# Fewer idle products in the last expert group, an earlier first sum over tokens, and a split first weight half

## The chip, the cores and the metric

One core of a Trainium2 chip runs the whole program. The metric is the device time of one execution in microseconds (us); less is better.

## What is computed

Two transformer blocks on one sequence of 256 tokens with 1024 features, all in float32. The first block mixes tokens (attention and a short convolution) and then runs a mixture of 32 SwiGLU experts: each token picks one of four router groups and two of the eight experts in it. The second block starts with a projection of the first block's result `x` onto five parts (q, k, v, u, z) of 512 columns each, and ends with a dense SwiGLU layer. Cut to the part that matters here:

```python
for g in range(N_GROUPS):
    act = silu(einsum('nd,edf->nef', h, w_gate[sl])) * einsum('nd,edf->nef', h, w_up[sl])
    act = act * combine[:, g, :, None]
    y = y + einsum('nef,efd->nd', act, w_down[sl])
x = x + y                                   # end of the first block
h = x @ w_in_2                              # start of the second: (256, 1024) @ (1024, 2560)
q, k, v, u, z = split(h, ...)
```

## The kernel before

**Experts.** The kernel takes the 32 experts four at a time: `group(g, ...)` runs eight times (g = 0 to 7; 7 is the last group, called `end` in the code). Each expert has room for 32 tokens, so that a group is one 128-wide gathered tile `xg`. A group's weights come as twelve tiles of 1 MB: eight "gu" tiles (gate and up columns, one for each 128 rows of the 1024 features, the loop over `kc`), and four "dn" tiles (the down projection: two column halves `c`, two row halves `f`). `by_expert` (L815) multiplies one weight tile by the four experts' tokens on TensorE (PE): L819. I call the tiles of the last group gu0 to gu7 and dn0 to dn3 (dn0 and dn1 make column half 0, dn2 and dn3 half 1).

After the eight gu tiles, ScalarE (ACT) and VectorE (DVE) make `h` (L848, L849), PE transposes it (L853), ACT copies it to `hT` (L854), and the dn tiles follow. The result of a column half is copied to `y` (half 0: ACT, L877; half 1 in the last group: ACT and DVE, a half each, L872 and L873). `to_tokens(c)` (L859, eight passes on PE) multiplies `y` by the group's scatter matrix and adds it onto four accumulators `acc` in PSUM, two feature chunks of 128 each: `acc[0]` and `acc[1]` get column half 0, `acc[2]` and `acc[3]` half 1. After the last group `acc` holds `x`, transposed.

**Idle products.** In the last group PE also runs products of the identity with itself into a bank that nobody reads (`warm`, L239): six (`WARM2`) after each of the eight gu tiles and six after dn0 and dn1. A float32 product of this kind shows as two passes in the trace.

**Start of the second block.** Its weights and `x` are used as sums of two float32r parts. `hi_lo` makes them: ACT copies the high part (L266), DVE subtracts for the low part (L267). `hi_lo_here` is the same at a fixed place in the order (L271, L272). `W.ahead(n)` splits weight units (half a tile, 128x1024) up to the n-th. PE's products of the projections are all on L284; the first one, z ("z2"), takes four units of 12 products each.

**Order and data.** PE, ACT and DVE run here in the order in which the code is written. All weight tiles come through one list on the SP queue (L79): a tile is issued as soon as a buffer is free and the transfer eight places before it has landed. Of the second block's tiles, z's first one is loaded in two halves of 512 KB.

Of the kernel before, what the change touches and what calls it, by code (L numbers as in the profile page):

```python
# [19 lines left out]
KD = D // P  # L20
# [14 lines left out]
WBUF = 3  # L35
WBUF2 = 9
WARM0 = 14
WARM1 = (18, 6)
WARM2 = 6

VEC = {}
_at = 0
# [84 lines left out]
def fused_blocks(ctx: ExitStack, tc: tile.TileContext, a, out):  # L127
# [10 lines left out]
    def pool(name, bufs=1, side=None, **kw):  # L138
        es = ExitStack()
        p = es.enter_context(tc.tile_pool(name=name, bufs=bufs, side=side, reuse_waits="tile", **kw))  # L140
        return es, p


    units_a, units_b, order = [], [], []
# [59 lines left out]
    def bank():  # L204
        return pa.tile([P, 512], F32, tag="a", name="pa_t")
# [7 lines left out]
    def bank_c():  # L213
        return pc.tile([P, 512], F32, tag="c", name="pc_t")
# [6 lines left out]
    feed = Feed(nc, order)  # L221
# [10 lines left out]
    ident = cp.tile([P, P], F32, name="ident")  # L232
    make_identity(nc, ident)

    def warm(new, n, x):

        z = new()[:, 0:P]
        for _ in range(n):
            tc.keep_in_program_order(mm(z, ident, x, start=True, stop=True))  # L239
# [25 lines left out]
    def hi_lo(hi, lo, src):  # L265
        act(hi, src, AF.Copy)  # L266
        tt(out=lo, in0=src, in1=hi.bitcast(F32), op=ALU.subtract)  # L267

    def hi_lo_here(hi, lo, src):

        tc.keep_in_program_order(act(hi, src, AF.Copy))  # L271
        tc.keep_in_program_order(tt(out=lo, in0=src, in1=hi.bitcast(F32), op=ALU.subtract))  # L272
# [31 lines left out]

    def proj_tok(W, name, xh, xl, then={}, new=bank):
        accs = [[new()] for _ in range(NT)]
        for u in range(4):
            hi, lo = W.get(name)
            for t in range(NT):
                dense_tok(accs[t], [(2 * u, hi, lo, 0), (2 * u + 1, hi, lo, 512)], (0,), xh, xl, t, u == 0, u == 3)  # L310
            if u in then:
                W.ahead(W.n_got + W.lead)
                then[u]()
        return [c[0] for c in accs]

    def rows_proj(W, name, acc, xh, xl, k0, first, last, then={}):

        if not last:
            for u in range(2):
                hi, lo = W.get(name)  # L320
                for t in range(NT):
                    dense_tok(acc[t], [(k0 + u, hi, lo, 0)], (0, 1), xh, xl, t, first and u == 0, False)
                if u in then:
                    W.ahead(W.n_got + W.lead)
                    then[u]()
            return
        ks = [(k0 + u,) + W.get(name, 2 * u) + (0,) for u in range(2)]
        for t in range(NT):
            for c in range(2):
                dense_tok(acc[t], ks, (c,), xh, xl, t, first, True)  # L330
                if 2 * t + c in then:
                    then[2 * t + c]()

    def four_banks():
        return [[bank(), bank()] for _ in range(NT)]
# [22 lines left out]
    def hb(x):  # L358
# [4 lines left out]
    xh, xl, at_hl, y_hl = [ringx.tile([P, 2048], F32, tag="w", name=n).bitcast(F32R).rearrange("p (k s) -> p k s", k=KD)  # L363
                           for n in ("xh", "xl", "at_hl", "y_hl")]
    ath, atl = at_hl[:, 0:4, :], at_hl[:, 4:8, :]
    yh, yl = y_hl[:, 0:4, :], y_hl[:, 4:8, :]
    wes, wp = pool("w_a", bufs=WBUF, side="left")
# [5 lines left out]
    c0, c1 = slice(0, 512), slice(512, D)  # L373
# [14 lines left out]
    W = Split(feed, wp, units_a, two_halves, WBUF)  # L388
# [190 lines left out]
    acc = None  # L579
    merged = {}  # L580
    with tc.manual_schedule(engines={mybir.EngineType.PE}):
        for i in range(4):
# [7 lines left out]
            for b, n, h_, l_ in ((1, "cv", yh, yl), (0, "sb", ath, atl)):  # L590
                z = bank_c()
                hi, lo = W.get(n)
# [10 lines left out]
            if i:  # L603
                acc = acc or four_banks()
# [168 lines left out]
    def scatter(g, pg):  # L773

        pc = pg.rearrange("p t (e s) -> p t e s", e=GE)
        tt(out=pc, in0=pc,
           in1=comb[:, :, GE * g:GE * g + GE].unsqueeze(3).to_broadcast([P, NT, GE, SLOT]), op=ALU.mult)
        st = dp.tile([P, S], F32, tag="st", name="st", bufs=2)
        zs = bank_c()[:, 0:S]
        for t in range(NT):  # L780
            tr(zs[:, t * P:(t + 1) * P], pc[:, t].rearrange("p e s -> p (e s)"), ident)
        act(st, zs, AF.Copy)
        return st
# [28 lines left out]
    acc = [bank().rearrange("p (k s) -> p k s", k=2) for _ in range(4)]  # L812
    slots = [slice(e * SLOT, (e + 1) * SLOT) for e in range(GE)]

    def by_expert(outs, x, w, start, stop):  # L815
        n = 512 // len(outs)
        for i, out in enumerate(outs):
            for e, sl in enumerate(slots):
                mm(out[sl, 0:n], x[:, sl], w[:, e * 512 + i * n:e * 512 + (i + 1) * n],  # L819
                   start=start, stop=stop, skip_group_check=True)  # L820
        feed.done(w)

    def group(g, pg, xg, some, st):
        end = g == NG - 1
        gu = bank_c()
        idle = bank_c() if end else None
        first = {0: ((0, 1), (1, 1)), 1: ((2, 2),), 2: ((4, 4),)} if g == 0 else {}
        for kc in range(KD):
            for k in first.get(kc, ()):
                some(*k)  # L830
            by_expert([gu], xg[:, kc, :], feed.get("gu"), kc == 0, kc == KD - 1)
            if end:
                warm(lambda: idle, WARM2, ident)
        if not end:
            if g == 0:
                st = scatter(0, pg)
            pg = picks(g + 1)
            xg, some = gather(pg)
            some(0, 4)
            some(4, 4)  # L840
            st_next = scatter(g + 1, pg)
        if g == 0:
            for kc in range(KD):
                for t in range(NT):
                    mm(acc[kc // 2][:, kc % 2, t * P:(t + 1) * P], xres[:, t, kc * P:(kc + 1) * P], ident,
                       start=kc % 2 == 0 and t == 0, stop=False, skip_group_check=True)
        h = dp.tile([P, 256], F32, tag="pr", name="h")
        act(h, gu[:, 0:256], AF.Silu)  # L848
        tt(out=h, in0=gu[:, 256:512], in1=h, op=ALU.mult)  # L849
        hT = dp.tile([P, 2, P], F32, tag="pg", name="hT")  # L850
        za = bank_c()[:, 0:256]
        for f in range(2):
            tr(za[:, f * P:(f + 1) * P], h[:, f * P:(f + 1) * P], ident)  # L853
        act(hT, za.rearrange("p (f s) -> p f s", f=2), AF.Copy)  # L854
        ys = []

        def to_tokens(c):
            for k in range(4):
                mm(acc[2 * c + k // 2][:, k % 2, :], ys[c][:, k * P:(k + 1) * P], st, start=False, stop=False,  # L859
                   skip_group_check=True)  # L860

        for c in range(2):
            zy = [bank_c() for _ in range(1 + (end and c))]
            for f in range(2):
                by_expert(zy, hT[:, f, :], feed.get("dn"), f == 0, f == 1)
                if c and not f:
                    to_tokens(0)
                elif end and not c:
                    warm(lambda: idle, WARM2, ident)
            y = dp.tile([P, 512], F32, tag="y", name="y")  # L870
            if c and end:
                act(y[:, 0:256], zy[0][:, 0:256], AF.Copy)  # L872
                nc.vector.tensor_copy(y[:, 256:512], zy[1][:, 0:256])  # L873
            elif c:
                nc.vector.tensor_copy(y, zy[0])  # L875
            else:
                act(y, zy[0], AF.Copy)  # L877
            ys.append(y)
        to_tokens(1)
        return None if end else (pg, xg, some, st_next)  # L880
# [59 lines left out]
    wes, wp = pool("w_b", bufs=WBUF2, side="left")  # L940
    xes, xp = pool("x_b", side="left")
    ees, ep = pool("blk2", side="right")
    W = Split(feed, wp, units_b, hi_lo_here, WBUF2, WBUF + 2)
    x_hl = xp.tile([P, 2, KD, S], F32R, name="x2")
    xh, xl = x_hl[:, 0], x_hl[:, 1]
    mh = xp.tile([P, KD, S], F32R, name="mh2")
# [161 lines left out]
    def then(*steps):  # L1108

        return {i: (lambda fs=fs: [f(*a) for f, *a in fs]) for i, fs in enumerate(steps)}  # L1110

    with tc.manual_schedule(engines=in_order):
        W.ahead(1)
        W.hi_lo = hi_lo
        for k in range(2):
            hi_lo(xh[:, k, :], xl[:, k, :], acc[0][:, k, :])
        W.ahead(2)
        for k in range(2, KD, 2):
            hi_lo(xh[:, k:k + 2, :], xl[:, k:k + 2, :], acc[k // 2])
        W.ahead(3)  # L1120
        for k in range(0, KD, 2):
            act(x2T[k // 4][:, k % 4:k % 4 + 2, :], acc[k // 2], AF.Copy)
        b2["z2"] = proj_tok(W, "z2", xh, xl, then([], [(x2_tok, 0, 0)], [(x2_tok, 0, 1)], [(x2_tok, 1, 0)]), bank_c)
# [30 lines left out]
    acc = four_banks()  # L1154
# [138 lines left out]
    acc = None  # L1293
# [8 lines left out]
    for i in range(12):  # L1302
# [11 lines left out]
        if 0 < i < 10:  # L1314
            acc = acc or four_banks()
# [111 lines left out]
```

## Time and profile before

| | us |
|---|---|
| median of 3 runs | 696.68 |
| lowest and highest | 695.07 and 699.05 |
| the profiled execution | 697.34 |
| its span, first to last instruction | 695.6 |

The profiled execution lies 1.74 us above its span and 0.66 us above the median. PE is busy for 656.5 us of the span (94%), DVE for 367.1 (53%), ACT for 270.2 (39%). PE's busy time counts the idle products too, so it does not tell how much of it was needed. The last expert group runs from about 365 to 397 us of the span.

### The profile page before, as it was taken

What the parts mean: (1) busy time and instruction counts of PE and PEld (TensorE: products, weight loads), DVE (VectorE), ACT (ScalarE), POOL (GpSimd) and SP (SyncE); (2) the same over time, 40 slices, a digit from 0 to 9 for tenths busy, and PEclk for the clock granted to TensorE, in tenths of its full rate; (3) what the DMA queues carried; (4) which work ended last, traced back from release to release, by engine and by line L of the source; (5) the groups of instructions that cost most, each with busy time, mean ns of one, the idle gap of its engine ahead of it and who ended that gap; (6) DMA issues with size and microseconds to landing.
All of it is one profiled execution on the core that took longest, in us unless ns stands there. A gap on an engine that the chain in (4) does not pass through costs nothing. (4 is left out here: it accounts for less than half of the span.)

```text
span 695.6 us, 10419 instructions
## 1 busy us (share of the span) xinstructions
PE 656.5 (94%) x4249; PEld 512.9 (74%) x4249; DVE 367.1 (53%) x578; ACT 270.2 (39%) x413; POOL 44.8 (6%) x60
## 2 busy tenths in 40 slices
PE   7999999999999989888679999999899999999995
PEld 6888999999856444344246688877788888888884
DVE  6666565554542021121010189867569966666636
ACT  6567654444401000000000294576347544444410
POOL 2222100000100000000000007101100000000001
PEclk9999999999999999999999999999999999999998
DMA  8983379737979999999999976742118865555001
GB/s 333 410 363 122 122 268 357 283 122 291 392 310 398 422 418 420 419 419 419 412 419 419 399 254 217 288 157 73 49 62 305 311 229 182 182 182 181 1 1 60
DMA packets 27558, 185.62 MB, mean 267 GB/s; under 512 B 3312, under 2 KB 3824, under 8 KB 5872
## 3 DMA queue, kind: packets, MB, share of 16 engines
q1 hardware_dynamic: 27504, 184.89, 68.3%
q8 instruction: 35, 0.57, 0.3%
q14 instruction: 19, 0.16, 0.1%
HBM read 183.83 MB, written 1.05 MB: 266 GB/s over the span
## 5 line engine op out<-in xcount | busy, mean ns | idle before, releaser
L267 DVE TENSOR_TENSOR wlo<-w,whi 128x1024 fp32r<-128x1024 f32 (+1 forms) x147 | 180.9, 1239 | 79.0 <-ACT whi L266 78.9
L266 ACT ACTIVATE whi<-w 128x1024 fp32r<-128x1024 f32 (+1 forms) x147 | 153.7, 1056 | 151.6 <-PE pa_t L284 55.0
L299 PE MATMUL pc_t<-x,whi 128*128 128x512 f32 x320 | 113.7, 399 | 0.0
L300 PE MATMUL pc_t<-x,wlo 128*128 128x256 f32 x320 | 89.9, 281 | 0.0
L299 PEld LDWEIGHTS pc_t<-x,whi 128*128 128x128 f32 x320 | 60.1, 188 | 15.0 <-issue 0.2
L819 PE MATMUL pc_t<-w,xg 128*32 128x512 f32 x512 | 60.3, 610 | 5.8 <-PEq L891 5.0
L300 PEld LDWEIGHTS pc_t<-x,wlo 128*128 128x128 f32 x320 | 60.4, 189 | 0.7 <-DVE wlo L267 0.4
L769 DVE TENSOR_TENSOR xg<-pc_t,vec 128x512 f32<-128x512 f32 (+2 forms) x18 | 11.4, 632 | 80.8 <-PE pc_t L768 80.8
L848 ACT ACTIVATE h<-pc_t 128x256 f32<-128x256 f32 x8 | 3.1, 382 | 110.9 <-PE pc_t L768 86.2
L819 PEld LDWEIGHTS pc_t<-w,xg 128*32 128x32 f32 x512 | 15.4, 111 | 39.0 <-issue 33.9
L284 PE MATMUL pa_t<-whi,x 128*128 128x512 f32 x128 | 41.9, 397 | 0.0
L859 PEld LDWEIGHTS pa_t<-st,y 128*128 128x128 f32 x128 | 23.0, 189 | 21.9 <-DVE y L875 12.5
L859 PE MATMUL pa_t<-st,y 128*128 128x256 f32 x128 | 31.9, 392 | 6.3 <-DVE y L875 6.2
L819 PE MATMUL pc_t<-w,hT 128*32 128x512 f32 (+1 forms) x272 | 32.8, 598 | 4.1 <-ACT hT L854 4.1
L293 PE MATMUL pc_t<-xh,wlo 128*128 128x256 f32 x128 | 36.2, 283 | 0.0
L292 PE MATMUL pc_t<-xl,whi 128*128 128x256 f32 x128 | 36.2, 283 | 0.0
L291 PE MATMUL pc_t<-xh,whi 128*128 128x256 f32 x128 | 36.2, 283 | 0.0
L768 PEld LDWEIGHTS pc_t<-pr,xres 128*128 128x128 f32 x256 | 29.3, 192 | 7.8 <-PE pc_t L819 4.2
L875 DVE COPY y<-pc_t 128x512 f32<-128x512 f32 x7 | 4.8, 692 | 52.3 <-PE pc_t L819 52.3
L768 PE MATMUL pc_t<-pr,xres 128*128 128x128 f32 x256 | 31.1, 279 | 0.9 <-DVE pr L759 0.9
L284 PE MATMUL pa_t<-whi,fh 128*128 128x512 f32 x88 | 28.6, 394 | 0.4 <-ACT whi L271 0.4
L284 PE MATMUL pa_t<-wlo,fh 128*128 128x512 f32 x88 | 28.6, 392 | 0.0
(315 smaller groups left out, 1228.1 us busy)
## 6 DMA issues: line engine op xcount, KB each, us to landing
w<-in_w_gu_dram SPq DMA_DIRECT2D x64, 1024.0 KB, 19.9
w<-in_w_dn_dram SPq DMA_DIRECT2D x32, 1024.0 KB, 19.9
w<-in_w_in_dram SPq DMA_DIRECT2D x28, 1024.0 KB, 12.6
w<-in_w_ffn_dram SPq DMA_DIRECT2D x22, 1024.0 KB, 5.1
w<-in_w_fdn_dram SPq DMA_DIRECT2D x11, 1024.0 KB, 4.9
w<-in_w_out_dram SPq DMA_DIRECT2D x8, 1024.0 KB, 4.9
w<-in_w_in_dram SPq DMA_DIRECT2D x4, 512.0 KB, 12.6
w<-in_w_cv_dram SPq DMA_DIRECT2D x2, 1024.0 KB, 9.1
```

The source lines that it names most:

```text
L266: act(hi, src, AF.Copy)
L267: tt(out=lo, in0=src, in1=hi.bitcast(F32), op=ALU.subtract)
L284: mm(acc[c], x_[:, kc, tok], w_[:, o + c * 512:o + (c + 1) * 512], start=first and i == 0 and n == 0, stop=last and i == len(ks) - 1 and n ...
L291: mm(acc, hi[:, f], xh[:, kc, :], start=kc == 0, stop=False)
L292: mm(acc, hi[:, f], xl[:, kc, :], start=False, stop=False)
L293: mm(acc, lo[:, f], xh[:, kc, :], start=False, stop=kc == nk - 1)
L299: mm(z, hi[:, f], x[:, :, kc, :], start=kc == 0, stop=False, skip_group_check=True)
L300: mm(z[:, 0, :], lo[:, f], x[:, 0, kc, :], start=False, stop=kc == nk - 1, skip_group_check=True)
L768: mm(zv[:, k, :], xres[:, t, kc * P:(kc + 1) * P], pr[:, t, :], start=t == 0, stop=t == 1)
L769: tt(out=xg[:, ks, :], in0=zv, in1=V("ffn_g")[:, ks].unsqueeze(2).to_broadcast([P, n, P]), op=ALU.mult)
L819: mm(out[sl, 0:n], x[:, sl], w[:, e * 512 + i * n:e * 512 + (i + 1) * n], start=start, stop=stop, skip_group_check=True)
L859: mm(acc[2 * c + k // 2][:, k % 2, :], ys[c][:, k * P:(k + 1) * P], st, start=False, stop=False, skip_group_check=True)
```

## The change

Three edits. (1) In the last group the idle products are kept only after gu4 to gu7, four after each instead of six; none stand after gu0 to gu3, dn0 and dn1. That is 16 instead of 60. (2) In the last group `to_tokens(0)` stands in front of dn2, not between dn2 and dn3. (3) At the start of the second block the first feature chunk of `x` is split in front of z's first weight unit, and that unit is split in two halves of 512 columns instead of one piece of 1024.

```diff
-WARM2 = 6
+WARM2 = 4
...
             by_expert([gu], xg[:, kc, :], feed.get("gu"), kc == 0, kc == KD - 1)
-            if end:
+            if end and kc >= KD // 2:
                 warm(lambda: idle, WARM2, ident)
...
             for f in range(2):
+                if end and c and not f:
+                    to_tokens(0)
                 by_expert(zy, hT[:, f, :], feed.get("dn"), f == 0, f == 1)
-                if c and not f:
+                if c and not f and not end:
                     to_tokens(0)
-                elif end and not c:
-                    warm(lambda: idle, WARM2, ident)
...
-    W = Split(feed, wp, units_b, hi_lo_here, WBUF2, WBUF + 2)
+    def halves_here(hi, lo, src):
+        for c in (c0, c1):
+            hi_lo_here(hi[:, c], lo[:, c], src[:, c])
+
+    W = Split(feed, wp, units_b, halves_here, WBUF2, WBUF + 2)
...
     with tc.manual_schedule(engines=in_order):
+        hi_lo(xh[:, 0, :], xl[:, 0, :], acc[0][:, 0, :])
         W.ahead(1)
         W.hi_lo = hi_lo
-        for k in range(2):
-            hi_lo(xh[:, k, :], xl[:, k, :], acc[0][:, k, :])
+        hi_lo(xh[:, 1, :], xl[:, 1, :], acc[0][:, 1, :])
         W.ahead(2)
```

`c0` and `c1` are the column halves 0 to 512 and 512 to 1024, which other code already uses.

PE's order in the last group, from gu7's idle products on (`pc_t` are banks for results, `pa_t` the accumulators, `w,xg` a gu tile and `w,hT` a dn tile; a pair of passes counts as one product here):

```order
-L239 MATMUL pc_t<-ident 128x128 x6
+L239 MATMUL pc_t<-ident 128x128 x4
 L853 MATMUL pc_t<-ident,h 128x128 x2
-L819 MATMUL pc_t<-w,hT 32x512 x4
-L239 MATMUL pc_t<-ident 128x128 x6
-L819 MATMUL pc_t<-w,hT 32x512 x4
-L239 MATMUL pc_t<-ident 128x128 x6
-L819 MATMUL pc_t<-w,hT 32x256 x8
+L819 MATMUL pc_t<-w,hT 32x512 x8
 L859 MATMUL pa_t<-st,y 128x256 x4
-L819 MATMUL pc_t<-w,hT 32x256 x8
+L819 MATMUL pc_t<-w,hT 32x256 x16
 L859 MATMUL pa_t<-st,y 128x256 x4
```

dn0 and dn1 now follow each other, and the first sum over tokens stands ahead of both dn2 and dn3.

ACT's order where the second block starts, before (`y` is the last copy of the expert stage, `pa_t` the accumulators, `x_5643` and `x_5599` the split `x`, `whi` the high part of a weight unit):

```order
L872 ACTIVATE y<-pc_t 128x256
L271 ACTIVATE whi<-w 128x1024
L266 ACTIVATE x_5643<-pa_t 128x256 x2
L266 ACTIVATE whi<-w 128x1024
L266 ACTIVATE x_5643<-pa_t 128x512 x3
```

and in the changed kernel:

```order
L872 ACTIVATE y<-pc_t 128x256
L266 ACTIVATE x_5599<-pa_t 128x256
L271 ACTIVATE whi<-w 128x512 x2
L266 ACTIVATE x_5599<-pa_t 128x256
L266 ACTIVATE whi<-w 128x1024
L266 ACTIVATE x_5599<-pa_t 128x512 x3
```

The first piece of `x` moved ahead of the weight unit, which is now two pieces. DVE's order changes in the same way; the orders of the SP queue and of GpSimd (POOL) stay as they were.

## Rows read from the trace of the kernel before

**Rows 1.** The page, part 2: what the DMA engines moved in 40 slices.

```profile
GB/s 333 410 363 122 122 268 357 283 122 291 392 310 398 422 418 420 419 419 419 412 419 419 399 254 217 288 157 73 49 62 305 311 229 182 182 182 181 1 1 60
```

**Rows 2.** The chain that ended last, 340 to 440: start us, us, what.

```profile
383.26 0.99 PE pc_t L819 x8
384.26 1.54 PE pc_t L239 x12
...
386.55 1.07 PE pc_t L819 x8
387.61 1.53 PE pc_t L239 x12
...
392.68 1.92 PE pa_t L859 x8
...
397.73 6.35 PE pc_t L284 x24
...
414.05 16.34 PE pa_t L284 x72
```

**Rows 3.** Timeline of the SP queue, 320 to 440: start us, us, what.

```profile
339.34 17.73 SPq L79 DMA_DIRECT2D w<-in_w_gu_dram  x8
359.29 9.36 SPq L79 DMA_DIRECT2D w<-in_w_dn_dram  x4
370.81 5.31 SPq L79 DMA_DIRECT2D w<-in_w_in_dram  x3
...
385.78 30.46 SPq L79 DMA_DIRECT2D w<-in_w_in_dram  x8
```

**Rows 4.** DMA issues from 346 to 357.2: KB each, us to landing.

```profile
w<-in_w_gu_dram SPq DMA_DIRECT2D x5, 1024.0 KB, 21.4
```

**Rows 5.** DMA issues from 363 to 369.

```profile
w<-in_w_dn_dram SPq DMA_DIRECT2D x3, 1024.0 KB, 19.9
```

**Rows 6.** DMA issues from 370.5 to 371.2.

```profile
w<-in_w_in_dram SPq DMA_DIRECT2D x1, 512.0 KB, 18.7
```

**Rows 7.** DMA issues from 385.5 to 390.

```profile
w<-in_w_in_dram SPq DMA_DIRECT2D x3, 1024.0 KB, 12.6
```

**Rows 8.** Timeline of PE, 224 to 262: a whole gu stage without idle products.

```profile
225.53 7.07 PE L819 MATMUL pc_t<-w,xg 128*32 128x512 f32 x64
```

**Rows 9.** Timeline, 340 to 381: in brackets, the idle time before and what ended it.

```profile
346.80 1.06 PE L819 MATMUL pc_t<-w,xg 128*32 128x512 f32 x8 [0.81 <-DMA w<-in_w_gu_dram]
```

**Rows 10.** Timeline of all engines, 380 to 440: the turn from the experts to z.

```profile
390.21 0.60 ACT L877 ACTIVATE y<-pc_t 128x512 f32<-128x512 f32 x1 [3.72 <-PE pc_t L819]
...
394.53 1.07 PE L819 MATMUL pc_t<-w,hT 128*32 128x256 f32 x16
...
395.30 0.38 ACT L872 ACTIVATE y<-pc_t 128x256 f32<-128x256 f32 x1 [4.49 <-PE pc_t L819]
395.58 1.05 ACT L271 ACTIVATE whi<-w 128x1024 fp32r<-128x1024 f32 x1
...
396.67 1.22 DVE L272 TENSOR_TENSOR wlo<-w,whi 128x1024 fp32r<-128x1024 f32 x1 [0.50 <-ACT whi L271]
...
397.94 0.19 PEld L284 LDWEIGHTS pc_t<-wlo,x 128*128 128x128 f32 x1 [0.40 <-DVE wlo L272]
...
399.49 1.56 ACT L266 ACTIVATE x<-pa_t 128x512 fp32r<-128x512 f32 x3
...
409.47 1.13 ACT L266 ACTIVATE whi<-w 128x1024 fp32r<-128x1024 f32 x1
```

**Rows 11.** Stretches: us, busy by engine, then PEclk (granted clock), DMA share, GB/s.

```profile
334.70:338.10 3.40, 0.02 (x3) 0.05 (x4) 0.00 (x0) 0.00 (x0) 0.00 (x0) 1.00 1.02 395
338.10:341.50 3.40, 3.40 (x17) 0.96 (x21) 0.00 (x0) 0.00 (x0) 0.00 (x0) 0.50 1.01 417
...
351.80:355.20 3.40, 0.85 (x4) 0.40 (x4) 1.31 (x3) 0.88 (x3) 0.00 (x0) 1.00 1.00 417
355.20:358.60 3.40, 3.19 (x16) 0.79 (x20) 0.00 (x0) 0.16 (x1) 0.00 (x0) 0.50 1.02 422
```

## Prediction

> **What bounds the kernel now.** I read the DMA rate by slices first: about 419 GB/s in nearly every slice from 226 us on, still 399 at 382 to 400 us, and falling only after that [rows 1]. So the expert stage runs beside a stream of 1 MB tiles that has no gap. Then the chain of waits: in the last group it is TensorE alone, one tile's products (0.99 us) and six idle products (1.54 us) in turn, 2.53 us a pair [rows 2]. From the last pair, which starts at 383.26, seven pairs back, gu0 starts at 365.5. PE thus bounds this stage, but at the very pace of the stream: eight gu tiles were issued over 17.73 us, the last at 339.34+17.73-0.33 = 356.7 (0.33 is one issue), 2.49 us apart [rows 3]. The question is how far behind the data PE runs, because removing PE work buys no more than that distance.
>
> Landings are issue plus time to landing. gu3 is the fourth issue: 339.34+3x2.49+21.4 = 368.2; gu7: 356.7+21.4 = 378.1 [rows 3, 4]. The dn tiles: dn0 359.29+21.4 = 380.7, dn3 368.3+19.9 = 388.2, dn1 and dn2 2.5 apart before that, 383.2 and 385.7 [rows 3, 5]. z's first half tile: 370.81+18.7 = 389.5 [rows 3, 6]. PE uses gu7 at 383.26, 5.1 us after it landed, and dn3 at 394.53, 6.3 us after [rows 2, 10]. No product of the last group waits for data today; there are 5 to 6 us to win and then the stream is the bound.
>
> **The change part by part.** *Idle products.* 44 of 60 go; one costs 1.54/6 = 0.257 us [rows 2], 11.3 us of PE in all. That is not the gain. Without them a gu tile costs 7.07/8 = 0.88 us [rows 8]. gu0, gu1 and gu2 have landed before PE gets to them, so PE is through them at 365.5+3x0.88 = 368.1, and gu3 lands at 368.2. From there each tile starts when it lands, as one already did at 346.80 after 0.81 us of waiting [rows 9], and four idle products (1.03) plus the tile (0.88) fit into 2.49. So the gu stage ends with gu7 starting at 378.1.
>
> From gu7's start to dn0's took 386.55-383.26 = 3.3 us [rows 2]; PE's transposes stood behind the six idle products, and with two fewer it is 2.8 to 3.3. dn0 starts at 381.0 to 381.4 and has landed (380.7). dn1 lands at 383.2. Its copy to `y` ended 390.21+0.60-389.14 = 1.7 us after dn1's start (389.14 is the end of the idle products behind dn0) [rows 2, 10], now 384.9.
>
> *The first sum over tokens* (1.92 us [rows 2]) now runs 384.9 to 386.8, in the time in which PE would wait for dn2 and dn3; dn2 (1.0 us) ends at 387.8, 0.4 before dn3 lands at 388.2. In the old place the sum would follow dn2 (385.7 to 386.7), end at 388.6 and hold dn3 up by 0.4. So the move is worth about 0.4, contained in what follows. What queues behind its wait for `y` on PE is dn2 alone, and that has slack. Together: dn3 starts at 388.2 and not at 394.53: **-6.3 us**.
>
> *Start of z.* From dn3's start to the first z product is 397.73-394.53 = 3.2 us, the last copies and the second sum [rows 2, 10]; unchanged, so z may start at 391.4. Its first 24 products took 6.35 us, while 72 later ones took 16.34, 5.45 for 24 [rows 2]: 0.90 us of waits, such as 0.40 for the low part of the first weight unit [rows 10]. In the new order ACT copies `y` until 388.2+0.77+0.38 = 389.4, then the first piece of `x` (0.38, taken like L872, the same size) to 389.8, then the half unit (1.56/3 = 0.52 for 512 columns) to 390.3; it landed at 389.5. DVE's half (1.22/2 = 0.61) ends at 391.0, before the second product wants it at 391.6. The second half unit, the second piece of `x` and the next unit follow at such distances; the tightest is the low part of chunks 2 and 3, ready near 394.2 for a product at about 394.6. So 0 to 0.9 us of waits go; I take **-0.7**, nearer to the full value, because every piece is ready in time on paper but by 0.4 us or less.
>
> *The rest.* One more instruction each on ACT and DVE: 2x0.52 for 1.05, 2x0.61 for 1.22 [rows 10], nothing. No DMA moves. z is followed by work bound by PE (72 products without a gap [rows 2]), which moves up as a whole. Its cover is weight tiles: q's first one lands at 385.78+12.6 = 398.4, whatever PE does [rows 3, 7], and PE, after z's 48 products, needs its parts at about 391.4+4x2.73 = 402.3 or later. Split, it can be ready at 398.4+1.05+1.22 = 400.7 [rows 10]. If that cover were gone, it would cost what the ACT rival below says.
>
> **Sum.** -6.3-0.7 = -7.0 (bounds -6.3 and -7.2): span 695.6 to 688.6, the profiled execution 697.34 to **690.3**. That execution lies 0.66 over the median of 696.68. I don't take the 0.66 off: what differs before 365 us on PE (the half-clock stretches below) is swallowed by the wait for gu3, and the stream sets the end. Against the median the gain is 6.4 us, 0.9%. About 0.5%, 3.5 us, is what a measurement of this kernel can tell from no change.
>
> **Rivals.** *The clock falls once or twice.* The granted clock was 0.50, 1.2 GHz in place of 2.4, at 338.1 to 341.5, after PE had stood almost still (0.02 us busy), and at 355.2 to 358.6, after 0.85 us of work in 3.4 us [rows 11]. The change puts waits of up to 1.6 us between tiles. For a fall speaks the thin stretch around dn1; against it, that no new stretch is as empty as the two in the rows. While PE waits for data a half clock costs little; between 384.9 and z, where PE has no room, 3.4 us at half speed cost up to 1.7 us. One fall there gives 692.0, two 693.7.
>
> *ACT waits, in its order, for q's and k's tiles.* Three tiles from 385.78 on land at 398.4 and then one per 2.5 us, the third at 403.4 [rows 3, 7]. ACT took that tile at 409.47 [rows 10]; 7.0 earlier would be 402.5, too soon, and the evictions that stand behind it are late. Estimated price 0.9 to 2 us where PE has no slack left: 691.2 to 692.3. Against it: PE consumes a tile in 5.5 us, the stream brings one in 2.5.
>
> *The clock falls at the first wait and stays down up to z; slower.* From gu3 on PE has 5x0.88 + 16x0.257 + 0.4 (transposes) + 4x1.0 + 2x1.92 = 16.8 us of work at full speed. At half speed a tile with four idle products takes 3.8 us, more than the 2.49 of the stream, so PE is the bound again: 33.6 us from 368.2 and some 2.5 us of copies, z at 404.3 instead of 397.73, **703.9** with nothing else lost. It decides from 14 us at the half level on, where the 7.0 are eaten up. For it: the tiles are now shorter than their waits. Against it: both half-clock stretches of the rows ended after 3.4 us of dense products, and at half speed this stage is dense. The Trainium skill has a rule that makes this the expected case ("TensorE: Matmul & The Clock Gate", section "HAM oscillation — how this bites in real kernels"): where a tile's products are shorter than the wait for the next tile, the clock drops in the wait and every tile begins slow. By that rule the answer is 703.9, by the rows 690.3. The trace has just one such wait, 0.81 us at 346.80, and the clock stayed at 1.00 through it.
>
> That the change doesn't do what it says is excluded by the order of the instructions.
>
> **How the numbers follow.** Forecast 0.68, its own range 688.5 to 692 (the bounds of the sum, and runs that spread by 1.6 below and 2.4 above their median). One or two falls 0.17, of which 0.05 end within 0.5%. ACT's wait 0.08, 0.01 of it within. Slower 0.05. Something I don't see eats most of it: 0.02, within. So faster 0.68+0.12+0.07 = 0.87, same 0.08, slower 0.05. The range goes from 687.8 (the larger bound and a low run) to 693.7 (two falls).
>
> **What the changed profile would show.** Right: gu3 to gu7 and dn1 and dn3 each with idle time before them that a DMA ended; dn3 at 388.2; the first sum in front of dn2; 24 z products in about 5.6 us from 391.4 on; the DMA rate as before up to 390; granted clock 1.00 from 365 to 400. Wrong: dn3 starting well after its landing, PEclk of 0.50 in that stretch, new waits of PE on ACT or DVE after 400, or a stream that lands later than before.

## The result and the profile after

The changed kernel takes 690.32 us (median of 4 runs, 689.87 to 691.09), the kernel before 696.45 in the same comparison (695.07 to 699.05). The ratio is 0.9896, with a 95% interval of 0.9874 to 0.9918: faster by 6.1 us. The forecast was 690.3. The profiled execution took 690.30, its span 688.6, 7.0 less than before.

The page of the changed kernel, parts 1 and 2, to be read beside the busy times of the kernel before and its DMA rate [rows 1]:

```profile
span 688.6 us, 10246 instructions
...
PE 645.1 (94%) x4161; PEld 502.8 (73%) x4161; DVE 367.5 (53%) x579; ACT 270.3 (39%) x414; POOL 45.7 (7%) x60
...
GB/s 332 412 375 123 123 243 363 306 127 255 406 286 406 420 419 421 418 420 417 415 419 422 414 388 190 301 123 121 3 62 338 324 193 185 183 189 178 0 1 61
```

The stream still moves about 419 GB/s up to 396 us (414 to 422 in the slices from 224 us on). PE's busy time fell by 11.4 us, about the 44 idle products; the time fell by little more than half of that.

The SP queue and the issues of dn2 and dn3 in the changed kernel, as [rows 3, 5] of before:

```profile
358.42 9.26 SPq L79 DMA_DIRECT2D w<-in_w_dn_dram  x4
...
384.80 13.14 SPq L79 DMA_DIRECT2D w<-in_w_in_dram  x5
...
w<-in_w_dn_dram SPq DMA_DIRECT2D x2, 1024.0 KB, 19.9
```

dn3 was issued at 358.42+9.26-0.33 = 367.35 and landed at 387.25. In the profile of before it landed at 388.22, so 0.97 of the 7.0 is a stream that happened to be ahead in that execution. Over the 13 traces of this study that landing lies anywhere from 385.97 to 390.29. I therefore measure everything behind it from dn3's landing on.

PE in the last group of the changed kernel (start us, us, instruction; in brackets the idle time before it and what ended it), as [rows 2, 9, 10] of before:

```profile
364.76 3.64 PE L819 MATMUL pc_t<-w,xg 128*32 128x512 f32 x32
...
369.81 1.06 PE L819 MATMUL pc_t<-w,xg 128*32 128x512 f32 x8 [1.41 <-DMA w<-in_w_gu_dram]
370.81 1.16 PE L239 MATMUL pc_t<-ident 128*128 128x128 f32 x8
372.30 1.06 PE L819 MATMUL pc_t<-w,xg 128*32 128x512 f32 x8 [0.34 <-DMA w<-in_w_gu_dram]
...
377.29 1.06 PE L819 MATMUL pc_t<-w,xg 128*32 128x512 f32 x8 [0.34 <-DMA w<-in_w_gu_dram]
...
382.28 1.07 PE L819 MATMUL pc_t<-w,hT 128*32 128x512 f32 x8 [0.92 <-DMA w<-in_w_dn_dram]
384.06 1.99 PE L859 MATMUL pa_t<-st,y 128*128 128x256 f32 x8 [0.72 <-ACT y L877]
385.98 1.07 PE L819 MATMUL pc_t<-w,hT 128*32 128x256 f32 x16
387.29 1.07 PE L819 MATMUL pc_t<-w,hT 128*32 128x256 f32 x16 [0.23 <-DMA w<-in_w_dn_dram]
388.49 1.99 PE L859 MATMUL pa_t<-st,y 128*128 128x256 f32 x8
390.13 0.58 PE L284 MATMUL pc_t<-whi,x 128*128 128x512 f32 x1
```

gu0 to gu3 run in one piece, and from gu4 on a DMA ends PE's waits for tiles (gu4 to gu7, dn1 and dn3). The first sum (384.06) stands in front of dn2 (385.98). dn3 starts 0.04 us after it landed, where before PE was 6.31 behind. The first z product follows dn3 by 2.85 (2.82 to 2.85 in all runs).

Stretches of the changed kernel (us, busy time of PE, PEld, DVE, ACT, POOL, then granted clock, DMA share, GB/s):

```profile
365.40:380.00 14.60, 11.93 (x94) 5.26 (x86) 0.42 (x1) 0.53 (x2) 0.00 (x0) 1.00 1.02 422
380.00:390.20 10.20, 7.91 (x65) 4.12 (x65) 1.69 (x4) 2.98 (x8) 0.00 (x0) 1.00 1.01 411
```

The clock stayed at 1.00. So far all went as forecast. The next lines did not: pieces of the chain of waits of the changed kernel from dn3 on (start us, us, what),

```profile
384.80 12.58 DMA w<-in_w_in_dram
...
397.40 1.07 ACT whi L266
...
398.50 2.37 DVE wlo L267 x2
...
419.20 1.69 POOL z L1012
...
420.96 2.14 POOL z L1013
...
423.15 2.00 PE pc_t L1019 x16
```

and where that PE row stands in the timeline of the changed kernel, then of before:

```profile
423.15 2.00 PE L1019 MATMUL pc_t<-z,w 128*128 128x64 f32 x16 [0.88 <-POOL z L1013]
```

```profile
427.71 2.15 POOL L1009 TENSOR_TENSOR z<-z,w 128x512 f32<-128x512 f32 x1
...
430.23 1.89 PE L1015 MATMUL pc_t<-z,w 128*128 128x64 f32 x16
```

L1019 is `z_mix`, the spatial product of z, which the kernel places between two steps of the projection of k. It needs z, normalised: gelu on ACT (L991), statistics on DVE, scale and shift on POOL (L1012, L1013). Before, POOL was done at 429.86, 0.37 us ahead of the product. Now PE stands still for 0.88 us until POOL is done. The gelu of z in the kernel before:

```profile
411.91 0.60 ACT L987 ACTIVATE z<-pc_t 128x512 f32<-128x512 f32 x1
```

**Where the time went**, from dn3's landing to the end: 307.39 us before, 301.33 after, a gain of 6.06. PE's lag behind dn3 gives -6.27. z's first 24 products (first z product to L965's first transpose) took 5.66 instead of 6.54: -0.88. From there to `z_mix` it took 27.35 instead of 26.32: +1.03 given back. The remaining 0.06 lies behind `z_mix`. The 1.03 fits the chain: counted from the landing, gelu starts at 17.88 (405.13-387.25) and no longer at 23.69 (411.91-388.22), and POOL's end came forward by the same 5.8. PE came forward by 7.15; of the 1.35 between them 0.37 was slack, and about 1.0 is the price.

### The profile page after: what moved, and what is told of

Same layout as the page of the kernel before. It is cut to its first block, busy times and chain, and to the rows that moved or that the text cites. A ratio compares the mean times of both kernels' runs of the same rounds, so it can differ in the third digit from the quotient of the medians.

```text
span 688.6 us, 10246 instructions
## 1 busy us (share of the span) xinstructions
PE 645.1 (94%) x4161; PEld 502.8 (73%) x4161; DVE 367.5 (53%) x579; ACT 270.3 (39%) x414; POOL 45.7 (7%) x60
## 4 chain that ended last, share of the span: by engine, by line
PE 66%; DMA 24%; DVE 4%; issue 2%; ACT 2%; POOL 1%; POOLq 0%; SPq 0%; DVEq 0%; ACTq 0%
PE pa_t L284 22%; DMA w<-in_w_gu_dram 12%; PE pc_t L299 10%; DMA w<-in_w_dn_dram 9%; PE pc_t L300 5%; DMA w<-in_w_in_dram 4%; PE pc_t L293 3%; PE pc_t L292 3%; PE pc_t L291 3%; PE pc_t L819 3%; PE pc_t L768 2%; PE pa_t L291 1%; PE pa_t L293 1%; PE pa_t L292 1%; PE pa_t L859 1%
## 5 line engine op out<-in xcount | busy, mean ns | idle before, releaser
L769 DVE TENSOR_TENSOR xg<-pc_t,vec 128x512 f32<-128x512 f32 (+2 forms) x18 | 11.4, 633 | 80.0 <-PE pc_t L768 80.0
```

What stands on the lines that cost most here:

```text
L769: tt(out=xg[:, ks, :], in0=zv, in1=V("ffn_g")[:, ks].unsqueeze(2).to_broadcast([P, n, P]), op=ALU.mult)
```

## Experiments

The theories: *S*, the lag behind the stream is the gain and edit 1 alone removes it. *W*, a wait on z's chain gives part of it back, and that chain is now set by the weight tiles that ACT splits in front of gelu. The rival to S is that the moved sum and the split carry shares of their own; the rival to W is that PE's own earlier work sets when POOL is done, and the rival on the clock is that the number of idle products matters. The table has each run's ratio to the kernel before in the same comparison, and of its trace, which is one execution: dn3's start behind its landing (lag), the time of z's first 24 products, PE's idle time in front of `z_mix`, POOL's end of z (L1013) counted from dn3's landing, and landing to the end of the span.

| | ratio [95%] | lag | z, 24 | idle | POOL | to the end |
|---|---|---|---|---|---|---|
| before | | 6.31 | 6.54 | 0 | 41.64 | 307.39 |
| after | 0.9896 [0.9874, 0.9918] | 0.04 | 5.66 | 0.88 | 35.84 | 301.33 |
| r1_again | 0.9909 [0.9887, 0.9930] | 0.04 | 5.68 | 2.01 | 37.01 | 302.53 |
| r2_idle_only | 0.9930 [0.9911, 0.9950] | 0.54 | 6.54 | 0 | 35.88 | 301.59 |
| r3_no_move | 0.9919 [0.9899, 0.9940] | 0.56 | 5.67 | 0.35 | 35.86 | 301.41 |
| r4_no_split | 0.9912 [0.9892, 0.9933] | 0.04 | 6.80 | 0 | 35.85 | 301.44 |
| r5_six | 0.9888 [0.9859, 0.9918] | 0.04 | 5.68 | 0.74 | 35.84 | 301.32 |
| r6_none | 0.9908 [0.9876, 0.9941] | 2.47 | 5.66 | 0 | 36.73 | 302.67 |
| r7_mix_later | 0.9869 [0.9848, 0.9891] | 0.04 | 5.66 | 0 | 37.05 | 300.20 |
| r8_lead | 0.9875 [0.9854, 0.9897] | 0.04 | 5.68 | 0.14 | 35.23 | 300.70 |
| r9_move_only | 1.0008 [0.9987, 1.0028] | 6.23 | 6.53 | 0 | 41.54 | 307.33 |
| r10_split_only | 0.9981 [0.9963, 0.9998] | 6.48 | 5.67 | 0 | 40.83 | 306.75 |
| r11_later_before | 1.0003 [0.9983, 1.0023] | 6.95 | 6.53 | 0 | 42.29 | 308.03 |

The intervals of r1 to r8 overlap almost all with each other, so what tells them apart is one trace of each. How far such a stretch repeats can be seen where the code is the same: from dn3's start to the end before, r9 and r11 took 301.08, 301.11 and 301.08. The largest difference between two executions of one kernel is that of a late tile: the 1.2 us between after and r1. The lag of the kernels that keep all 60 idle products differs as well, from 6.23 to 6.95.

**r1_again** is the changed kernel once more, unchanged, beside the next three.

> The changed kernel again, as it is, to stand beside the partial ones. My theory of its gain: PE ran 6.3 us behind the weight stream at the last down tile (dn3) and now waits for it; the first 24 products of z lost 0.85 us of waits; and 1.0 us is given back at z's spatial product, which waits for GpSimd because ScalarE's evictions of z stand behind splits of q's tiles that arrive when the stream brings them. Expected 690.3 us, and in the trace dn3 starting within 0.1 us of its landing and an idle time of about 0.9 us of PE in front of z's spatial product that GpSimd ends. A rival, that the landmarks differ from execution to execution by as much as these terms, expects the wait before the spatial product to be gone or doubled.

Measured: 691.02 against 697.46, a gain of 6.4. PE in front of `z_mix`, and ACT ahead of gelu (L991):

```profile
424.92 2.00 PE L1019 MATMUL pc_t<-z,w 128*128 128x64 f32 x16 [2.01 <-POOL z L1013]
```

```profile
404.57 1.06 ACT L266 ACTIVATE whi<-w 128x1024 fp32r<-128x1024 f32 x1 [1.07 <-DMA w<-in_w_in_dram]
405.65 1.28 ACT L991 ACT_TABLE_LOAD   x1
406.95 0.60 ACT L991 ACTIVATE z<-pc_t 128x512 f32<-128x512 f32 x1
```

and the same place in the profile of the changed kernel shown above:

```profile
399.90 1.06 ACT L266 ACTIVATE whi<-w 128x1024 fp32r<-128x1024 f32 x1 [0.48 <-DMA w<-in_w_in_dram]
...
402.77 1.06 ACT L266 ACTIVATE whi<-w 128x1024 fp32r<-128x1024 f32 x1
403.84 1.28 ACT L991 ACT_TABLE_LOAD   x1
405.13 0.60 ACT L991 ACTIVATE z<-pc_t 128x512 f32<-128x512 f32 x1
```

ACT's order puts gelu behind the split of the first unit of k's first tile. In r1 that tile landed at 404.55, 4.05 us after the tile before it instead of some 2.5. Counted from dn3's landing it came 1.58 later than in the changed kernel, gelu 1.20 later, POOL's end 1.17, and the wait at `z_mix` is 2.01 instead of 0.88: most of a late tile goes into PE's idle time. This speaks for W. In the changed kernel ACT did not stand still for this tile: it landed at 402.36 and was split at 402.77. ACT's last wait there is for q's second tile (399.90), and from it to gelu ACT works without a pause. Where no tile is late, the chain is thus the landings of q's tiles and 5.2 us of ACT's own work behind them.

**r2_idle_only**: edit 1 alone.

```diff
-                if end and c and not f:
-                    to_tokens(0)
                 by_expert(zy, hT[:, f, :], feed.get("dn"), f == 0, f == 1)
-                if c and not f and not end:
+                if c and not f:
                     to_tokens(0)
...
-    W = Split(feed, wp, units_b, halves_here, WBUF2, WBUF + 2)
+    W = Split(feed, wp, units_b, hi_lo_here, WBUF2, WBUF + 2)
...
-        hi_lo(xh[:, 0, :], xl[:, 0, :], acc[0][:, 0, :])
         W.ahead(1)
         W.hi_lo = hi_lo
-        hi_lo(xh[:, 1, :], xl[:, 1, :], acc[0][:, 1, :])
+        for k in range(2):
+            hi_lo(xh[:, k, :], xl[:, k, :], acc[0][:, k, :])
```

> The first edit alone: idle products as in the changed kernel, the sum between dn2 and dn3, z's first unit unsplit. Theory: dn3 starts 0.4 us after its landing, z's first 24 products keep 0.9 us of waits, so that z's end is 1.3 us later than in the changed kernel; but the spatial product is held by the evictions and GpSimd anyway, which swallows up to 1.0 of it: 690.3 to 690.7 us, with the idle time ahead of the spatial product gone. Rival, that the three edits add up: 690.3 + 0.4 + 0.85 = 691.6 us.

Measured: 692.34. By the trace 301.59 to the end, 5.80 less than before and only 0.26 more than with all three edits. dn3 starts 0.50 later and z's products take 0.88 longer than in the changed kernel, and yet gelu starts at 17.92 and POOL ends at the same 35.88. PE reaches `z_mix` without a wait:

```profile
422.23 1.89 PE L1013 MATMUL pc_t<-z,w 128*128 128x64 f32 x16
```

So edit 1 carries 5.80 of the 6.06. PE's z products, 1.38 later at their end, did not move POOL's end: the rival to W falls. In after and in r2 to r5 gelu starts 17.88 to 17.92 after dn3's landing.

**r3_no_move**: the changed kernel with the first sum back between dn2 and dn3 (the first part of the diff above).

> The changed kernel with the first sum over tokens back between dn2 and dn3. Theory: dn3 starts 0.4 us later than its landing, z's products all 0.4 us later, and the wait in front of the spatial product shrinks by that: 690.3 us. Rival, adding up: 690.7 us.

Measured: 691.49. PE at that place:

```profile
385.25 1.07 PE L819 MATMUL pc_t<-w,hT 128*32 128x256 f32 x16 [1.64 <-DMA w<-in_w_dn_dram]
386.25 1.99 PE L859 MATMUL pa_t<-st,y 128*128 128x256 f32 x8
388.18 1.07 PE L819 MATMUL pc_t<-w,hT 128*32 128x256 f32 x16
```

The sum holds dn3 up by 0.56, as worked out ahead (0.4). It then comes out of the wait at `z_mix`, 0.35 instead of 0.88: 0.08 is left at the end.

**r4_no_split**: the changed kernel without edit 3 (the rest of the diff above).

> The changed kernel with z's first weight unit unsplit and ahead of x, as before. Theory: dn3 at its landing, 0.85 us of waits back in z's first 24 products, swallowed by a wait of only some 0.1 us in front of the spatial product: 690.3 to 690.5 us. Rival, adding up: 691.2 us.

Measured: 691.90. z's first 24 products take 6.80, 1.14 longer, and the wait at `z_mix` is gone with it; 0.11 is left at the end.

```profile
424.80 1.89 PE L1015 MATMUL pc_t<-z,w 128*128 128x64 f32 x16
```

**r5_six** and **r6_none**: the number of idle products after gu4 to gu7.

```diff
-WARM2 = 4
+WARM2 = 6
```

> The changed kernel with six idle products in place of four after gu4 to gu7: 24 in place of 16. Theory: a tile with six takes 0.88 + 1.54 = 2.42 us and the stream brings one in 2.49, so dn3 still starts within 0.1 us of its landing and from that landing to the end of the span nothing changes (301.3 us in the first profile of the change). Rival, that the gain goes by the number of products taken off PE, 0.257 us each: eight more cost 2.1 us, dn3 starts that much after its landing.

```diff
             by_expert([gu], xg[:, kc, :], feed.get("gu"), kc == 0, kc == KD - 1)
-            if end and kc >= KD // 2:
-                warm(lambda: idle, WARM2, ident)
```

> The changed kernel without any idle product in the last group. Theory: PE waits longer for each tile, dn3 starts at its landing, and from there to the end 301.3 us again, as long as the clock stays up. Rival, the clock: it falls to 1.2 GHz in the stretch from gu4 to dn1 (PEclk 0.50), dn3 starts late by up to 1.7 us, and z's first products take twice as long for a while.

With six the time to the end is 301.32, the same. Two more per tile only fill PE's wait:

```profile
375.90 1.61 PE L239 MATMUL pc_t<-ident 128*128 128x128 f32 x12
377.44 1.07 PE L819 MATMUL pc_t<-w,xg 128*32 128x512 f32 x8
```

Without any, the granted clock falls to 0.50, 1.2 GHz, for 10.2 us. The stretches of r6, with the columns as above, and PE's rows from gu6 on:

```profile
366.00:380.00 14.00, 9.64 (x75) 3.11 (x72) 0.69 (x1) 0.37 (x1) 0.00 (x0) 1.00 1.01 421
380.00:390.20 10.20, 8.42 (x30) 3.41 (x34) 0.42 (x1) 1.00 (x3) 0.00 (x0) 0.50 1.02 417
390.20:396.00 5.80, 5.66 (x50) 4.04 (x42) 3.78 (x7) 4.35 (x10) 0.64 (x1) 1.00 1.03 411
```

```profile
376.00 1.06 PE L819 MATMUL pc_t<-w,xg 128*32 128x512 f32 x8 [1.43 <-DMA w<-in_w_gu_dram]
378.50 1.06 PE L819 MATMUL pc_t<-w,xg 128*32 128x512 f32 x8 [1.44 <-DMA w<-in_w_gu_dram]
...
381.75 3.67 PE L819 MATMUL pc_t<-w,hT 128*32 128x512 f32 x16 [0.53 <-ACT hT L852]
386.13 3.78 PE L857 MATMUL pa_t<-st,y 128*128 128x256 f32 x8 [0.72 <-ACT y L875]
389.85 2.10 PE L819 MATMUL pc_t<-w,hT 128*32 128x256 f32 x32
```

gu6 and gu7 still run at full speed behind waits of 1.43 and 1.44; the clock falls at 380.0, in the wait behind gu7. The first sum takes 3.78 instead of 1.99, and dn3 starts 2.47 after its landing. 1.34 of it is left at the end (302.67 against 301.33), because the wait at `z_mix` swallows the rest. Here PE is late enough to set POOL's end (36.73). The median of r6 is 692.89; one of its four executions took 689.52, with a mean clock of 0.988 over the span, as the changed kernel has it (0.987 to 0.991), against 0.977 to 0.982 in the others. The fall was shorter or absent in that one, of which there is no trace.

**r7_mix_later**: the changed kernel with `z_mix` of the first token half one step later, behind the transposes of q.

```diff
-    b2["k2"] = proj_tok(W, "k2", xh, xl, then([(rope, "q2", 1, True), (z_scale, 0)], [(z_scale, 1)], [(z_mix, 0)],
-                                              [(heads, qT)]))
+    b2["k2"] = proj_tok(W, "k2", xh, xl, then([(rope, "q2", 1, True), (z_scale, 0)], [(z_scale, 1)], [],
+                                              [(heads, qT), (z_mix, 0)]))
```

> The changed kernel with z's first spatial product one weight unit later on PE, behind the transposes of q instead of ahead of k's last unit. Theory: the 0.9 us (2.0 us in one execution) for which PE waited for GpSimd there go, so that from dn3's landing to the end it is 300.4 us and not 301.3 or 302.5. Rival, that the time given back belongs to the whole stage and shows up at the next wait: 301.3 us or more, with a new wait after it.

Measured: 689.59 (688.12 to 690.42), and 300.20 to the end, 1.13 less than after. k's first tile was late in this execution as in r1 (4.05 after the one before), gelu started 19.1 after dn3's landing in both, and POOL ended 37.05 after dn3's landing. Here it cost nothing; against r1, which had the same late tile, the end comes 2.33 earlier. ACT's row, and PE's:

```profile
405.18 1.06 ACT L266 ACTIVATE whi<-w 128x1024 fp32r<-128x1024 f32 x1 [1.07 <-DMA w<-in_w_in_dram]
...
426.06 1.04 PE L350 MATMUL pc_t<-ident,roped 128*128 128x128 f32 x8
426.93 1.90 PE L1019 MATMUL pc_t<-z,w 128*128 128x64 f32 x16
```

**r11_later_before** is the same edit on the kernel before.

> The kernel before with z's first spatial product one weight unit later, the edit that took 1.1 us off the changed kernel. Theory: PE does not wait there in the kernel before (GpSimd ends 0.4 us ahead of it), so nothing is gained: 307.4 us from dn3's landing to the end, a ratio of 1.000. Rival: the later place is better in itself, 306.3 us.

Measured: 698.03, ratio 1.0003. From dn3's start to the end it took 301.08, as in before. Where there was no wait, moving the product gains nothing: the wait is of the change's making.

**r8_lead**: the changed kernel with the weights split one unit less far ahead during z, so that gelu comes earlier in ACT's order.

```diff
+        W.lead -= 1
         b2["z2"] = proj_tok(W, "z2", xh, xl, then([], [(x2_tok, 0, 0)], [(x2_tok, 0, 1)], [(x2_tok, 1, 0)]), bank_c)
+        W.lead += 1
```

> The changed kernel with weights split four and not five units ahead during z, so that the first unit of k, whose tile lands 15.1 us after dn3, no longer stands ahead of the evictions of z on ScalarE. Theory: z's chain over ScalarE, VectorE and GpSimd ends about 1 us earlier than the 35.9 us after dn3's landing at which it ended in four of five profiles of kernels with the first edit, and most of the wait in front of the spatial product goes: 300.4 to 300.7 us from dn3's landing to the end. Rival, that this chain is held by its own length on VectorE and GpSimd: it ends at 35.9 again and nothing changes.

Measured: 689.73, and 300.70 to the end, 0.63 less than after.

```profile
405.44 1.28 ACT L991 ACT_TABLE_LOAD   x1
406.73 0.60 ACT L991 ACTIVATE z<-pc_t 128x512 f32<-128x512 f32 x1
```

dn3 landed at 390.29 in this execution, so gelu ran 16.44 after it, against 405.13-387.25 = 17.88: 1.44 earlier. POOL's end came forward by only 0.61 (35.23), so ACT's order is one link of the chain and DVE's order, where the low parts of the weights stand between z's statistics, another: between two steps of z's mean (L996 and L997 of the second half) stand three of them, 3.48 us, where the changed kernel has one of 1.22. How the remainder divides was not tried.

**r9_move_only** and **r10_split_only**: edit 2 alone and edit 3 alone on the kernel before (the hunks of the change).

> The kernel before with the second edit alone: the first sum over tokens in front of dn2, all 60 idle products kept. Theory: PE is still 6.3 us behind the stream at dn3, the copy to y is done before the idle products behind dn1 end, so only the order of two pieces of PE work changes: dn3 starts 6.3 us after its landing, from the landing to the end 307.4 us as before, a ratio of 1.000. Rival: the 0.4 us that the order is worth in the changed kernel shows here too, 307.0.

> The kernel before with the third edit alone: x's first piece ahead of z's first weight unit, and that in two halves. Theory: the 0.85 us of waits in z's first 24 products go (6.54 to 5.67 us), but GpSimd had only 0.4 to 0.5 us to spare in front of the spatial product, and z's chain moves up less than that because here ScalarE is not held by the stream: from dn3's landing to the end 306.6 to 306.9 us, against 307.4. Rival: the waits are covered by something else and nothing changes.

Measured: r9 698.18, no difference by time; from gu0's start to the end its trace has 329.85 against 330.13, 0.28 less, all of it ahead of dn3, whose products follow dn2's without a break. That is less than the 0.4 of the rival and more than the nothing of the theory, and one trace is all there is for it. r10 697.19, ratio 0.9981; z's first 24 products take 5.67, and dn3's start to the end 300.27 against 301.08. So edit 3 is worth 0.8 where POOL has not become the limit, and 0.11 behind edit 1 (r4).

**The best version** is r7, whose ratio lies below that of the changed kernel, with overlapping intervals; that it is faster rests on the traces (1.13 less than after, 2.33 less than r1).

## Why the prediction was right, and where it was not

**The idle products and the stream: right.** The step "removing PE work buys no more than that distance" gave -6.3 for 11.3 us of removed work; the lag went from 6.31 to 0.04, and edit 1 alone brings 5.80 (r2). r5 shows the other side of it: eight more idle products cost nothing, since PE waits for tiles there. In detail the first tile to wait was gu4, not gu3; gu7 to dn0 took 380.29-377.29 = 3.0 (forecast 2.8 to 3.3), dn1 to `y`'s copy 1.7 as forecast, and the wait in front of dn3 was 0.23 (0.4).

**The first sum: right in its place, almost nothing at the end.** Worth 0.52 at dn3 (0.56-0.04 in r3; forecast 0.4), 0.08 at the end.

**The start of z: right in its place, almost nothing at the end.** -0.88 for the forecast -0.7, so all of the waits went. At the end it is 0.11 (r4). The 3.2 us from dn3's start to z's first product were read from a row of the chain, which starts at 397.73; the product itself starts at 397.38, so it is 2.85, and the 24 products took 6.54 instead of 6.35. The two errors nearly cancel.

**"The rest ... moves up as a whole": the step that failed.** I took weight tiles for the only cover and checked whether PE would wait for q's parts. It did not. But z's chain runs over ACT, DVE and POOL, and it had 0.37 us to spare in front of `z_mix`. When PE moved up by 7.15 us, ACT's splits in front of gelu could follow by 5.8 only, since their tiles come with the stream, and POOL's end became fixed at 35.84 to 35.88 after dn3's landing (after, r2 to r5), whatever PE had gained. 1.03 went there. The rival "ACT waits, in its order" named this mechanism and its price of 0.9 to 2; it had a chance of 0.08, and was argued away by how PE consumes tiles, which says nothing on evictions that stand behind a tile in ACT's order. It came true beside the forecast, not in place of it: a wait at `z_mix` of 2.01 in r1, 0.88 in after, and 0 in r7. In r1 and r7 ACT waits for the tile that the rival names, k's first; in after ACT's work behind q's tiles is enough.

**Why the number still fits.** Measured from the landing the gain was 6.06, where the sum had -7.0. The profiled span fell by 7.0 because the stream was 0.97 ahead in that execution; the median fell by 6.1, against the forecast's 6.4 from the median. The forecast hit the time with one term missing and an execution of before that was slower than its median left in. The two errors cancel; that the time came out at 690.3 is luck in this part. The reason given for leaving the 0.66 in, that the stream sets the end, overlooks that the stream itself is not at the same place in every execution (387.25 against 388.22 here).

**The clock.** No fall, as the likeliest case had it. It is the 16 idle products that hold it: without them (r6) the case of falling clock came, and cost 1.34 by the trace. In r6 the products of a gu tile, 0.88, are shorter than the wait behind them (1.44 in front of gu7). For this the Trainium skill ("TensorE: Matmul & The Clock Gate", section "HAM oscillation — how this bites in real kernels") has the clock drop in each wait and each tile begin slow; its kernel waits longer than this one, 3 to 5 us. r6 agrees only in that such a stage lost the clock: gu6 and gu7 began at full speed, and the clock fell once. The forecast called that rule the expected case for the change, but by its own sums a tile with its four idle products (0.88+1.03) is longer than the wait behind it (0.58), and in the trace that wait is 0.34. The wait of 0.81 at 346.80 did not test the rule either, since it is shorter than a tile's 0.88. In r6 the clock does not stay down up to the end of z, as the rival had it for this change, but for 10.2 us; and in the changed kernel it did not drop though gu4 followed a wait of 1.41.

## What to carry to other kernels

In a stage that a data stream paces, measure how far each engine stands behind the landings: that lag, not the work removed, is what can be won, and edits that come behind it are swallowed (0.08 and 0.11 here for steps that won 0.5 and 0.9 to 1.1 in their place). Before one engine is moved up, follow every chain that leaves it and comes back over other engines, and write down the slack where it returns; a slack of 0.4 us under a move of 7 is the next wait. Where several executions start their stream at different times, compare from a landing on, not from the start of the span.

## What the runs showed of the hardware

Tiles of 1 MB land 2.49 us apart, but between gu0 and k's first tile ten of the 13 traces have an interval of 3.5 to 4.05 us: between gu0 and gu1 in eight (359.23 to 363.27 in before, 358.35 to 362.28 in after), in front of k's first tile in r1 (400.50 to 404.55) and r7 (401.11 to 405.16). In r2 the tile behind k's first is the late one (401.10 to 405.14). The queue was not idle. In r1's window of 4.0 us it moved on at the full rate:

```profile
400.60:404.60 4.00, 4.00 (x21) 3.31 (x20) 3.34 (x3) 2.93 (x5) 0.00 (x0) 1.00 1.01 412
```

At 412 GB/s that is 1.6 MB in the time in which one tile of 1 MB landed, so other transfers moved on meanwhile. A 16 KB packet of the instruction queue falls into it (at 401.9), but the changed kernel has such a packet at 401.6, between two tiles that landed 2.49 apart, so it does not suffice as the cause. Why the interval is longer, and what chooses its place, is not settled.

The clock in r6 stayed at 0.50 for 10.2 us though PE was busy for 8.42 of them; the half-clock stretches of before were 3.4 long [rows 11].
